# A segment-mean kernel: outputs shifted on chip to fixed addresses and stored plainly, tables built in stages between rows, part of the id sums on ScalarE

## The chip, the cores and the metric

The kernel runs on one core of a Trainium2 chip. The metric is device time in microseconds (us). PE is TensorE, DVE is VectorE, ACT is ScalarE, POOL is GpSimd, SP is SyncE; a trailing q (DVEq, SPq) means the engine's sequencer, which issues DMAs, waits and branches. Every run quoted here was with a granted clock of 1.0 where it was recorded.

## The reference

There are 10 million values with sorted segment ids; the result is the mean of each of 10,000 segments.

```
n, num_segments = 10_000_000, 10000
data = randn(n).astype(float32);  segment_ids = sort(randint(0, num_segments, n))
np.add.at(sums, segment_ids, data)
np.add.at(counts, segment_ids, 1)
return sums / np.maximum(counts, 1)
```

## The kernel before

Each of the 128 partitions takes 78,125 consecutive elements, cut into 98 rows of 800 (the last has 525). On this input a row holds at most one boundary between two segments. The kernel reads every 160th id, gathers by an indirect DMA the 159 ids around the boundary, and gets the boundary's place from their sum. Then, for each row, ACT sums the whole row and DVE sums the part before the boundary (the "split"). From these two numbers per row, small tables give the means.

```
def second_look(a, b):                      # per six rows: the sum of the gathered ids, on DVE
    def s1():
        nc.vector.tensor_reduce(
            out=GS[:, a:b], in_=gt32[:, s : s + b - a, 0 : 2 * W : 2], axis=AX.X, op=ALU.add)
    ...
def total(r):                               # ACT
    nc.scalar.activation(out=junk_a[:, 0:n], in_=d, func=ACT.Copy, accum_out=T[:, r : r + 1])
def split(r):                               # DVE
    nc.vector.scalar_tensor_tensor(
        out=junk_v[:, 0:n], in0=iota[:, 0:n], scalar=KK[:, r : r + 1], in1=d,
        op0=ALU.is_lt, op1=ALU.mult, accum_out=A[:, r : r + 1])
...
def write(o, i):                            # the output's address is in the data: AN
    nc.gpsimd.indirect_dma_start(
        out=out2d[:], out_offset=bass.IndirectOffsetOnAxis(ap=AN[:, i : i + 1], axis=0),
        in_=o[:], in_offset=None)
...
def branch():                               # a general path for inputs of another kind
    with tc.If(nc.values_load(badi[0:1, 0:1], min_val=0, max_val=1) > 0):
        general_path(...)                   # compiled in, never taken on this input
...
after[80].append(verdict)                   # is the fast path allowed?
after[84].append(branch)
after[84].append(tables_a)                  # rows below 66
after[96].append(tables_b)                  # the others but three; first write
...
for r in range(..., NR):
    total(r); split(r)
    for f in after[r]: f()
sums(95, 98); carry(95, 106); table2(); write(out2, 1)
```

A partition's first segment number depends on the data, so `write` stores each partition's 72 and then 8 outputs at addresses from `AN`. The verdict and the tables are three blocks of DVE work, put between the splits.

## Time and profile before

| what | us | where it is read |
|---|---|---|
| time | 214.97, median of 4 runs (214.14 to 215.08) | runs of the same rounds as the changed kernel |
| profiled span | 212.4 | page |
| DVE ends | 201.2 | timeline |
| DVE busy, ACT busy | 149.7, 95.4 | page |

These are lines of the page: the span, the busy time of each engine, the busy tenths in 40 slices of the span (5.3 us each), and the costliest groups (busy time and mean nanoseconds of one, then idle time before them and what ended it).

```profile
span 212.4 us, 1195 instructions
PE 1.6 (1%) x6; PEld 1.4 (1%) x6; DVE 149.7 (70%) x443; ACT 95.4 (45%) x197; POOL 102.2 (48%) x113
...
DVE  5425169848955984993886787589999888999800
ACT  2002047517624753762663664377876598000000
...
DMA  6699999999999999999999999999999990000000
...
L379 DVE SCALAR_TENSOR_TENSOR junk_v<-iota,q_116,data_t 128x800 bf16<-128x800 f32 x98 | 102.4, 1045 | 35.4 <-DMA data_t<-in_data_dram 34.5
L374 ACT ACTIVATE junk_a<-data_t 128x800 bf16<-128x800 f32 x98 | 85.0, 867 | 83.6 <-DMA data_t<-in_data_dram 79.8
L359 DVE TENSOR_REDUCE GS<-GT 128x6 f32<-128x954 int32 (+1 forms) x17 | 18.7, 1103 | 5.1 <-DMA GT<-in_segment_ids_dram,IDX 5.0
```

The DMA row is full up to slice 32, counted from 0 (about 175 us): until then the transfers can limit. DVE is at 8 or 9 tenths from slice 27 to slice 37, beyond the data's end: from about 145 us on DVE is the limit, and it carries a backlog past the last landing. The last two digits of its row are 0: for 11 us nothing computes. The windows view shows the three stretches: DVE is busy 26.7 of 40 us while data come, 9.9 of 10 us after their end, and 1.1 of the last 13; its columns are the stretch, its length, then busy time and count of PE, PEld, DVE, ACT and POOL, the clock, the DMA share and GB/s.

```profile
60.00:100.00 40.00, 0.00 (x0) 0.00 (x0) 26.71 (x72) 19.26 (x40) 22.62 (x24) 1.00 1.05 308
180.00:190.00 10.00, 0.00 (x0) 0.00 (x0) 9.86 (x22) 0.00 (x0) 0.00 (x0) 1.00 0.00 0
200.00:213.00 13.00, 0.00 (x0) 0.00 (x0) 1.14 (x4) 0.00 (x0) 1.24 (x2) 1.00 0.01 4
```

The end of the timeline (start, length, engine, line, operation, and in brackets the idle time before it), and the waits of the SP queue at the kernel's closing line (total us, times, longest):

```profile
200.84 0.40 DVE L582 TENSOR_REDUCE out_141<-sel_135 128x8 f32<-128x232 f32 x1
202.33 0.99 POOL L585 DMA_INDIRECT out_dram<-out_141,AN  x1 [2.09 <-issue]
```

```profile
SPq L703 <- DMA out_dram<-out_141,AN: 27.1, 1, 27.1
SPq L703 <- PEq L703: 6.9, 2, 6.4
```

DVE's last result is there at 201.2; POOL issues the last write at 202.3; it lands at 204.5. From 205.3 on SP waits 6.4 us in one piece, and the span ends at 212.4. The view names PE's sequencer as releaser of that wait.

### The profile page before, as it was taken

The numbers are of one execution on the slowest core, as the hardware profiler recorded it, in microseconds if no ns is written. First come the engines' busy times: TensorE is split into PE (matmuls) and PEld (weight loads), VectorE is DVE, ScalarE is ACT, GpSimd is POOL, SyncE is SP. The second block draws the span as 40 slices with busy tenths as digits, with TensorE's granted clock in tenths as the row PEclk, the third lists the DMA queues.
The fourth block names the chain that finished last, engine by engine and source line by source line (L and its number), as shares of the span: only waits on it lengthen the run. The fifth ranks groups of instructions, "written<-read, shape, count | busy, mean of one in ns | idle before, by whom it ended". The sixth has DMA issues, their size and how long they took to land. (4 is left out here: it accounts for less than half of the span.)

```text
span 212.4 us, 1195 instructions
## 1 busy us (share of the span) xinstructions
PE 1.6 (1%) x6; PEld 1.4 (1%) x6; DVE 149.7 (70%) x443; ACT 95.4 (45%) x197; POOL 102.2 (48%) x113
## 2 busy tenths in 40 slices
PE   0000000100000000000000000000000100000000
PEld 0000000100000000000000000000000000000000
DVE  5425169848955984993886787589999888999800
ACT  2002047517624753762663664377876598000000
POOL 4577756777777427707735752771674000000110
DMA  6699999999999999999999999999999990000000
GB/s 9 36 97 243 250 400 377 145 385 398 270 234 405 397 96 382 391 232 278 403 325 184 396 404 89 402 393 401 415 399 396 406 395 14 0 0 0 7 2 0
DMA packets 74733, 53.39 MB, mean 251 GB/s; under 512 B 65306, under 2 KB 65389, under 8 KB 74720
## 3 DMA queue, kind: packets, MB, share of 16 engines
q1 hardware_dynamic: 69952, 40.51, 66.3%
q0 software_dynamic: 4768, 12.78, 19.7%
q14 instruction: 13, 0.11, 0.1%
HBM read 56.46 MB, written 0.04 MB: 266 GB/s over the span
## 5 line engine op out<-in xcount | busy, mean ns | idle before, releaser
L379 DVE SCALAR_TENSOR_TENSOR junk_v<-iota,q_116,data_t 128x800 bf16<-128x800 f32 x98 | 102.4, 1045 | 35.4 <-DMA data_t<-in_data_dram 34.5
L345 POOL DMA_INDIRECT GT<-in_segment_ids_dram,IDX x98 | 97.9, 999 | 59.9 <-issue 26.5
L374 ACT ACTIVATE junk_a<-data_t 128x800 bf16<-128x800 f32 x98 | 85.0, 867 | 83.6 <-DMA data_t<-in_data_dram 79.8
L359 DVE TENSOR_REDUCE GS<-GT 128x6 f32<-128x954 int32 (+1 forms) x17 | 18.7, 1103 | 5.1 <-DMA GT<-in_segment_ids_dram,IDX 5.0
L585 POOL DMA_INDIRECT out_dram<-out_140,AN x1 | 1.0, 1016 | 37.1 <-DVE out_140 L556 37.1
L374 ACT ACTIVATION_READ_ACCUMULATOR junk_a<-data_t 128x1 f32 x98 | 18.3, 186 | 0.0
L379 DVE DVE_READ_ACCUMULATOR junk_v<-iota,q_116,data_t 128x1 f32 x98 | 8.2, 83 | 0.0
L306 DVE TENSOR_TENSOR eq<-pr 128x40 f32<-128x40 int32 (+3 forms) x11 | 2.1, 192 | 4.3 <-DMA pr<-in_segment_ids_dram 4.3
L364 DVE TENSOR_TENSOR kr<-QQ,GS 128x6 f32<-128x6 f32 (+1 forms) x17 | 2.7, 160 | 0.0
L367 DVE TENSOR_TENSOR q_116<-kr,q_116 128x6 f32<-128x6 f32 (+1 forms) x17 | 2.7, 160 | 0.0
L240 DVE CAST iota<-i_i 128x800 f32<-128x800 int32 x1 | 1.0, 995 | 1.7 <-POOL i_i L239 1.7
L315 DVE TENSOR_SCALAR ST<-jc 128x10 f32<-128x10 f32 (+3 forms) x11 | 2.1, 195 | 0.0
L308 DVE CAST q_116<-pr 128x11 f32<-128x11 int32 (+4 forms) x11 | 2.1, 188 | 0.0
L311 DVE TENSOR_REDUCE jc<-eq 128x10 f32<-128x40 f32 (+3 forms) x11 | 2.0, 186 | 0.0
L319 DVE TENSOR_SCALAR NB<-q_116 128x10 f32<-128x10 f32 (+3 forms) x11 | 2.0, 182 | 0.0
L585 POOL DMA_INDIRECT out_dram<-out_141,AN x1 | 1.0, 988 | 2.1 <-issue 2.1
L336 DVE SCALAR_TENSOR_TENSOR IDX<-NB,pos 128x10 int32<-128x10 f32 (+3 forms) x11 | 1.8, 165 | 0.0
L329 DVE TENSOR_TENSOR pos<-ST,wb 128x10 f32<-128x10 f32 (+3 forms) x11 | 1.8, 165 | 0.0
L330 DVE SCALAR_TENSOR_TENSOR QQ<-q_116,ST 128x10 f32<-128x10 f32 (+3 forms) x11 | 1.8, 161 | 0.0
L312 DVE TENSOR_TENSOR q_116<-q_116 128x10 f32<-128x10 f32 (+3 forms) x11 | 1.7, 158 | 0.0
L374 ACT ACT_TABLE_LOAD x1 | 1.3, 1283 | 0.8 <-PEq L692 0.8
L483 PE MATMUL badp<-bad,ones 128*128 128x1 f32 x2 | 0.6, 362 | 124.3 <-DVE bad L482 124.3
(93 smaller groups left out, 29.0 us busy)
## 6 DMA issues: line engine op xcount, KB each, us to landing
data_t<-in_data_dram SPq DMA_DIRECT2D x48, 800.0 KB, 13.5
GT<-in_segment_ids_dram,IDX POOLq DMA_INDIRECT x98, 6.1
data_t<-in_data_dram SPq DMA_DIRECT2D x1, 662.5 KB, 18.7
pr<-in_segment_ids_dram SPq DMA_DIRECT2D x7, 50.0 KB, 16.9
pr<-in_segment_ids_dram SPq DMA_DIRECT2D x1, 48.0 KB
pr<-in_segment_ids_dram SPq DMA_DIRECT2D x1, 40.0 KB, 5.7
pr<-in_segment_ids_dram SPq DMA_DIRECT2D x1, 30.0 KB, 5.1
pr<-in_segment_ids_dram SPq DMA_DIRECT2D x1, 21.0 KB, 3.3
```

The lines of the kernel that those rows point to most:

```text
L306: nc.vector.tensor_tensor(out=eq, in0=in0b, in1=in1b, op=ALU.is_equal)
L308: nc.vector.tensor_copy(out=V[:, a:e], in_=pr32[:, a:e, 0])
L311: nc.vector.tensor_reduce(out=jc, in_=eq, axis=AX.X, op=ALU.add)
L315: nc.vector.tensor_scalar(out=ST[:, a:b], in0=jc, scalar1=float(S), scalar2=float(1 + W), op0=ALU.mult, op1=ALU.add,)
L319: nc.vector.tensor_scalar(out=NB[:, a:b], in0=BT[:, a:b], scalar1=-1.0, scalar2=1.0, op0=ALU.mult, op1=ALU.add)
L345: nc.gpsimd.indirect_dma_start(out=GT[:, r % RING, :], out_offset=None, in_=ids2d[:], in_offset=bass.IndirectOffsetOnAxis(ap=IDX[:, r : r ...
L359: nc.vector.tensor_reduce(out=GS[:, a:b], in_=gt32[:, s : s + b - a, 0 : 2 * W : 2], axis=AX.X, op=ALU.add)
L364: nc.vector.tensor_sub(out=kr, in0=QQ[:, a:b], in1=GS[:, a:b])
L367: nc.vector.tensor_mul(out=KK[:, a:b], in0=kr, in1=BT[:, a:b])
L374: nc.scalar.activation(out=junk_a[:, 0:n], in_=d, func=ACT.Copy, accum_out=T[:, r : r + 1])
L379: nc.vector.scalar_tensor_tensor(out=junk_v[:, 0:n], in0=iota[:, 0:n], scalar=KK[:, r : r + 1], in1=d, op0=ALU.is_lt, op1=ALU.mult, accum_ ...
L585: nc.gpsimd.indirect_dma_start(out=out2d[:], out_offset=bass.IndirectOffsetOnAxis(ap=AN[:, i : i + 1], axis=0), in_=o[:], in_offset=None,)
```

## The change

The intent: take work off DVE, spread what stays into its idle time, and shorten the end. The core of the diff:

```
-    def write(o, i):
-        nc.gpsimd.indirect_dma_start(out=out2d[:], out_offset=...AN..., in_=o[:], in_offset=None)
+    def place(c0, c1):          # shift a partition's table by its own delta (0..12), by a mask
+        def s1(): nc.vector.tensor_tensor(out=shf[:, c0:c1, :], in0=view(tab[:, c0 : c0 + 1], [[1, n], [1, ND]]),
+                      in1=view(dm[:, 0:1], [[0, n], [1, ND]]), op=ALU.mult)
+        def s2(): nc.vector.tensor_reduce(out=own[:, c0:c1], in_=shf[:, c0:c1, :], axis=AX.X, op=ALU.add)
+    def late_out():             # after the last split: only the last 4 rows' terms
+        ...
+        nc.vector.tensor_reduce(out=OUT[:, CL:NO], in_=prodL, axis=AX.X, op=ALU.add)
+        for i, (src, dst) in enumerate(own_outputs(OUT, out2d[0:1, :])):      # four plain stores
+            (nc.scalar if i % 2 else nc.sync).dma_start(out=dst, in_=src)
+    def add_ids(r):             # rows below ON_ACT = 66
+        nc.scalar.activation(out=junk_a[:, 0:W], in_=gt32[:, r % RING, 0 : 2 * W : 2], func=ACT.Copy,
+                             accum_out=GS[:, r : r + 1])
...
-    after[CHECK_AT].append(verdict)
-    after[IF_AT].append(tables_a)
-    after[C2 + 1].append(tables_b)
+    put(46, counts(0, 48))
+    put(52, sums(0, 48) + table(0, 8))
+    put(70, counts(48, 72))
+    put(max(bounds[NG - 1] - X_LOOK, 0) + 5, keys(48, NX)[1:] + check(), 2)
+    IF_AT = 83
+    put(76, select(8, 13))
+    put(77, sums(48, 72) + table(8, 13) + place(0, 40), 2)
     after[IF_AT].append(branch)
+    put(IF_AT + 1, [first_out])
+    put(IF_AT + 2, select(13, NT1 // 4))
+    put(91, counts(72, NX), 3)
+    put(93, ext_sums() + late_select(), 6)
+    put(93, sums(72, RL) + table(13, NT1 // 4) + place(40, NO) + early_out(), 16)
```

`put` appends one step after one row, the next step after the next row, or a few at a time. Further: the gathers' look-ahead moves by two rows and that of the probes (every 160th id) by three, the last tile is loaded in two pieces, and the first six outputs have a store of their own (`first_out`).

## The prediction

> **What bounds the kernel now.** Up to about 144 us the transfers: the windows view gives a DMA share of 1.0 or more from 15 us on, with DVE busy 82%, 67%, 75% of 30-60, 60-100, 100-140 us; DVE and ACT wait for data_t (waits view: 34.5 and 79.8 us). From row 68 on (144.2 us) DVE: data come at about 1.1 us a row, a split costs DVE 1.09 us (timeline), so every other DVE op is lag never made good: verdict 161.9 to 167.4 (5.5 us), first tables 172.0 to 178.9 (7 us), second tables 193.2 to 198.9 (5.7 us), id sums 1.06 us per six rows. The last tile lands at about 177.4 us (issue 158.5 plus 18.7), but DVE ends at 201.2. Then the tail: 1.1 us until POOL issues, 1.0 us of POOL, 2.2 us to landing (205.5), 6.9 us of epilogue to 212.4.
>
> **What the change does.**
> 1. Id sums of rows 0 to 65 go to ScalarE: 11 reduces of 1.1 us off DVE, in the stage where DVE waits for data, so I credit about nothing. On ACT each costs an estimated 0.47 us (slope of its 800- and 525-column forms plus the accumulator read): 1.46 us a row with the total, against about 1.75 us a row of arriving data. ACT keeps up.
> 2. Verdict and tables are spread between splits. The work stays on DVE, but independent ops after a split start every 0.07 to 0.12 us instead of a dependent 0.2 or more. Tables of rows below 48 move into idle time.
> 3. New DVE work: shifting (two multiplies, two reduces of about 510 elements, 0.69 us each) and a 92-column table. Between rows 93 and 94 about 6.3 us still runs in one block.
> 4. The end after the last split falls to an estimated 1.3 us.
> 5. Plain stores replace the indirect write. [...] I take 2.6 us from DVE's end to landing instead of 4.3.
> 6. DMA bytes are unchanged; probes come a few rows later; data end within 1 us of 177.4.
>
> **The sum.** I replayed the new DVE order with durations and arrivals from the trace (the same replay of the old order ends at 199.6 plus 1.1 us of branch waits; true 201.2). DVE lag passes 4 us at row 75, 9 us at row 82, 12 us at row 93; DVE ends at about 197.5. DVE gains 3.7 us, the tail 1.7: 5.4 of the 24 us that DVE runs after the last tile. Span about 207, time **208.8 us**, range 205.3 to 211.8. Chances: faster by over 2% 0.77, within 2% 0.21, slower 0.02.
>
> **What would show it.** Timeline: row 68's split near 144 us; DVE without gaps after about row 70; a 6 us block of tables before the last four splits, near 185 to 191; DVE end 196 to 199; stores landing under 3 us later. Lines: id reduces on DVE about 6 us instead of 18.7; ACT busy about 125 us.
>
> **What would make it wrong.** Data earlier around rows 66 to 72 (gathers shift by two rows) end DVE earlier by as much. Interleaved small ops dearer than 0.1 us each, later. The two reads of the fallback tiles wait for the skipped branch's semaphores, which the DMA queue gives only as tiles 44 and 48 land (168.7 and 177.4 us): were DVE quicker than I think, it would stall there, and could not end below about 184. The epilogue may change without the POOL write.

The 2.6 us is the estimate; what the trace shows is 2.2 us from the start of the last indirect write's issue to its landing. The sum: 3.7 us of DVE and 1.7 us of tail (4.3 less 2.6) make 5.4 us, from a span of 212.4 us to about 207.

## The result

| | before | after |
|---|---|---|
| time, us | 214.97 (214.14 to 215.08) | 205.64 (205.27 to 205.75) |
| profiled span, us | 212.4 | 204.0 |
| DVE ends, us | 201.24 | 200.09 |
| DVE's end to the span's end, us | 11.2 | 3.9 |
| DVE busy, ACT busy, us | 149.7, 95.4 | 139.5, 124.2 |

The ratio is 0.9571, with a 95% interval of 0.9544 to 0.9598: faster. A ratio here is the mean time of one kernel's fast runs over that of the other's of the same rounds, so not quite the ratio of the medians. The lines that answer to those of before:

```profile
span 204.0 us, 1430 instructions
PE 1.6 (1%) x6; PEld 1.4 (1%) x6; DVE 139.5 (68%) x454; ACT 124.2 (61%) x329; POOL 100.3 (49%) x112
...
DVE  5520924864488488458748848884999997499992
ACT  2013497996499699679959847653779668910000
...
DMA  5699999999999999999999999999999999300000
...
L416 DVE SCALAR_TENSOR_TENSOR junk_v<-iota,q_121,data_t 128x800 bf16<-128x800 f32 x98 | 102.1, 1042 | 41.5 <-DMA data_t<-in_data_dram 37.0
L411 ACT ACTIVATE junk_a<-data_t 128x800 bf16<-128x800 f32 x98 | 85.0, 867 | 33.8 <-DMA data_t<-in_data_dram 27.8
L381 ACT ACTIVATE junk_a<-GT 128x159 bf16<-128x159 int32 x66 | 22.8, 346 | 20.5 <-DMA GT<-in_segment_ids_dram,IDX 18.6
```

Two things in the DVE row were not in the plan. Its last digit is 2, where before it had two zeros: the empty end is gone. And a 7 and a 4 stand between the nines, at slices 33 and 34 (168 to 178 us), in the middle of the stretch where DVE limits.

The timeline shows that dip as one hole, just after the branch over the fallback (L780). "issue" means that the profile shows nothing the engine waited for.

```profile
171.31 1.05 DVE L416 SCALAR_TENSOR_TENSOR junk_v<-iota,q_121,data_t 128x800 bf16<-128x800 f32 x1 [0.30 <-DVEq L780]
172.28 0.08 DVE L416 DVE_READ_ACCUMULATOR junk_v<-iota,q_121,data_t 128x1 f32 x1
172.28 0.21 DVE L730 SCALAR_TENSOR_TENSOR out_156<-tab,nflag,fb_158 1x6 f32<-1x6 f32 x1
176.14 1.05 DVE L416 SCALAR_TENSOR_TENSOR junk_v<-iota,q_121,data_t 128x800 bf16<-128x800 f32 x1 [3.65 <-issue]
...
199.74 0.35 DVE L747 TENSOR_REDUCE OUT<-prodL 128x21 f32<-128x189 f32 x1
```

So DVE, expected 3.7 us earlier, was 1.15 us earlier, and the end, expected 1.7 us shorter, was 7.3 us shorter (11.2 less 3.9). That the total still fell inside the predicted range is luck: one term was too large and the other too small. For the span 5.4 us of gain were predicted and 8.4 measured; for the time, 208.8 us and 205.64.

The end, in the SP queue's waits:

```profile
SPq L860 <- DMA out_dram<-OUT: 0.7, 2, 0.5
SPq L860 <- PEq L860: 0.7, 2, 0.5
```

The piece of 6.4 us is now 0.5. The groups of the closing line show what it was. Here the columns are count, minimum, median and maximum ns, and first and last start. The first fence is before, the second after:

```profile
L703 POOLq DRAIN  x3: 40/113/9161, 202.4 to 212.1; - x3
```

```profile
L860 POOLq DRAIN  x3: 40/107/8077, 167.2 to 203.7; - x3
```

In both kernels POOL ends its program with one long DRAIN, of 9161 and 8077 ns. Before, it began at 202.4 us, with the last indirect write, and the whole core waited for it until 211.6. After, POOL's last work is a gather that ends at 164.2 us and its part of the branch, up to 167.2; its DRAIN runs from 167.2 to 175.3 us, where nobody waits for it.

### The profile page after: what moved, and what is told of

The parts are those of the page before. It is cut to its first block, busy times and chain, and to the rows that moved or that the text cites. A ratio compares the mean times of both kernels' runs of the same rounds, so it can differ in the third digit from the quotient of the medians.

```text
span 204.0 us, 1430 instructions
## 1 busy us (share of the span) xinstructions
PE 1.6 (1%) x6; PEld 1.4 (1%) x6; DVE 139.5 (68%) x454; ACT 124.2 (61%) x329; POOL 100.3 (49%) x112
## 5 line engine op out<-in xcount | busy, mean ns | idle before, releaser
L381 ACT ACTIVATE junk_a<-GT 128x159 bf16<-128x159 int32 x66 | 22.8, 346 | 20.5 <-DMA GT<-in_segment_ids_dram,IDX 18.6
L381 ACT ACTIVATION_READ_ACCUMULATOR junk_a<-GT 128x1 f32 x66 | 12.3, 186 | 0.0
L400 DVE TENSOR_TENSOR kr<-QQ,GS 128x6 f32<-128x6 f32 (+2 forms) x17 | 2.7, 161 | 10.8 <-ACT junk_a L381 10.8
L394 DVE TENSOR_REDUCE GS<-GT 128x6 f32<-128x954 int32 (+2 forms) x6 | 6.2, 1032 | 0.0
L403 DVE TENSOR_TENSOR q_121<-kr,q_121 128x6 f32<-128x6 f32 (+2 forms) x17 | 2.8, 167 | 0.0
L673 DVE TENSOR_REDUCE tab<-sel 128x32 f32<-128x384 f32 (+2 forms) x3 | 1.6, 534 | 0.1
```

What stands on the lines that cost most here:

```text
L381: nc.scalar.activation(out=junk_a[:, 0:W], in_=gt32[:, r % RING, 0 : 2 * W : 2], func=ACT.Copy, accum_out=GS[:, r : r + 1],)
L394: nc.vector.tensor_reduce(out=GS[:, c:e], in_=gt32[:, s : s + e - c, 0 : 2 * W : 2], axis=AX.X, op=ALU.add)
L400: nc.vector.tensor_sub(out=kr, in0=QQ[:, a:b], in1=GS[:, a:b])
L403: nc.vector.tensor_mul(out=KK[:, a:b], in0=kr, in1=BT[:, a:b])
```

## The experiments

Theory for the end: the 7 us came from POOL's closing DRAIN, because POOL no longer issues the last DMA. Rival: any plain store has a short end for another reason (fewer waits on the write, a shorter POOL program). Theory for the hole, a guess that no view shows: the DVE's instruction stream is being refilled after the jump over the fallback (below: the "refill"). Rivals: the store of the first outputs, or the small operation before it, stalls DVE; or the interleaved operations do. Times are medians; ratios are to the kernel before in the same rounds (its medians were 214.3, 213.9, 214.0 and 214.2 us in the four batches).

### One small store of the changed kernel issued by POOL

```
-            (nc.scalar if i % 2 else nc.sync).dma_start(out=dst, in_=src)
+            [nc.sync, nc.scalar, nc.sync, nc.gpsimd][i].dma_start(out=dst, in_=src)
```

> The changed kernel with the smallest of its four last stores (15 elements) issued on GpSimd's queue instead of ScalarE's. Theory (the end of the program waits for a GpSimd drain of 8 to 9 us that starts after GpSimd's last DMA; in the kernel before it ran from 202.4 to 211.6 us, in the changed one from 167.2 to 175.3, out of sight): the drain moves to about 201.5 to 210, the span grows by 6 to 7.5 us, time 211.5 to 213. Rival (the end became short because the scatter by index and its descriptors went, or because one wait per store is cheap): time within 1 us of 205.6.

Measured: 211.66 us (211.11 to 212.01), ratio 0.9865 (0.9838 to 0.9891). Only one store of 15 values changed its queue, and 6 us came back. The drain and SP's wait:

```profile
L860 POOLq DRAIN  x3: 44/113/8753, 200.6 to 210.0; - x3
```

```profile
SPq L860 <- PEq L860: 6.9, 2, 6.4
```

The wait of 6.4 us is back to the tenth. DVE's end hardly moved (200.4 against 200.1). So the end depends on when POOL issues its last DMA, and not on the write being indirect.

### The kernel before, with plain stores and nothing else

Wrong results: the two stores go to fixed addresses without the shift.

```
-        nc.gpsimd.indirect_dma_start(...AN...)
+        nc.sync.dma_start(out=bass.AP(z.tensor, z.offset + off, [[c, n], [1, c]]), in_=o[0:n, :])
```

> The kernel before with its two indirect writes replaced by two plain stores of the same tiles to fixed addresses on the sync queue. Result wrong on purpose (outputs land at shifted addresses). Theory (the tail is nearly the whole gain): DVE still ends near 201.2, stores land by 204, no drain behind them; span about 204.7, time 206 to 207.5, that is almost all of the change's 9.3 us. Rival, my prediction (the store is worth 1.7 us, DVE's work the rest): time 212.5 to 213.5.

Measured: 205.59 us (205.40 to 206.16), ratio 0.9598 (0.9572 to 0.9623). That is the time of the whole change, and a little under what I had expected. DVE ends at 201.1 as before; the span is 203.7.

```profile
L702 POOLq DRAIN  x3: 40/107/8077, 169.0 to 203.5; - x3
```

So moving the last write off POOL is worth nearly all of the net gain. All the rest of the change, for which the page counts 235 more instructions, paid back what it cost and no more. Why, the next runs tell.

### Without the branch

```
-    after[IF_AT].append(branch)
```

> The changed kernel without the conditional fallback (this data never takes it, so the result stays right). Theory (the 3.65 us hole of DVE at 172.5 to 176.1 us is an instruction refill after the jump over the fallback[...]): the hole goes, with the 0.3 us of the branch itself; DVE ends near 196.2 instead of 200.1, time 201.3 to 202. Rival (the hole is a wait of the small first_out operation's tile or store): the hole stays, time within 0.7 us of 205.6.

Measured: 203.38 us (202.91 to 204.97), ratio 0.9511 (0.9464 to 0.9559). The hole is gone; DVE ends at 196.7. I had expected 201.3 to 202; data came later in this run (row 68's split at 143.8 us, against 143.2), its end took 4.4 us instead of 3.9, and its times scatter more than others. The branch is needed for the hole; this run alone doesn't tell how it makes it.

### The first outputs' store moved away from the branch

```
-    put(IF_AT + 1, [first_out])
+    put(92, [first_out])
```

> The changed kernel with the small first_out operation and its store moved from after row 84 to after row 92; the branch stays at row 83. Refill theory: a hole of 3 to 4 us stays, at nearly the same time (about 172 to 176) and one or two instructions further on; time within 0.5 us of 205.6. Rival (first_out's waits make the hole): no hole at 172 us, time 201.5 to 202.5 if it doesn't come back at row 92.

Measured: 205.75 us (204.93 to 206.54), ratio 0.9585 (0.9554 to 0.9615). The hole stays, now between a split and the read of its own accumulator:

```profile
174.02 1.05 DVE L416 SCALAR_TENSOR_TENSOR junk_v<-iota,q,data_t 128x800 bf16<-128x800 f32 x1
177.75 0.08 DVE L416 DVE_READ_ACCUMULATOR junk_v<-iota,q,data_t 128x1 f32 x1 [2.68 <-issue]
```

These two are one line of the kernel, and no operand of another engine or DMA lies between them. The rival falls: the store of the first outputs isn't the cause. What stays the same is the count of instructions behind the jump: the fourth one stalls in both kernels.

### No id sums on ScalarE

```
-ON_ACT = 66
+ON_ACT = 0
```

> The changed kernel with all id sums back on DVE (one number: 66 to 0). My prediction credited the move of rows 0 to 65 with about nothing, as DVE waits for data there: row 68's split stays within 0.7 us of 143.2, DVE's end within 0.7 us of 200.1, time 205 to 206.5, with about 12 us more DVE busy time. Rival (the move is worth its 12 us of DVE work, or a good part): time 208 or more.

Measured: 202.15 us (201.91 to 202.83), ratio 0.9459 (0.9438 to 0.9479). This missed: I expected no gain over the change (ratio 0.9571), and it is 1.2% faster. The hole is gone, although the branch is there, and DVE ends at 195.8 with 10.6 us more work (busy 150.1). The edit adds 11 reduces, with their waits, ahead of the branch; it moves every later instruction of DVE along.

### More id sums on ScalarE

```
-ON_ACT = 66
+ON_ACT = 90
```

> The changed kernel with the id sums of rows 66 to 89 on ScalarE too (66 to 90). These four reduces of 1.06 us stand in the stage where DVE is the limit, so all of it should count: DVE ends 4.2 us earlier, near 195.9, time 201 to 202. ScalarE pays about 24 times 0.47, 11 us, and has slack; if it becomes the limit instead, DVE waits for its totals before the late tables and the gain is under 2 us.

Measured: 200.11 us (199.69 to 200.33), ratio 0.9356 (0.9341 to 0.9372), DVE's end 194.0, which is 1 to 2 us better than expected. With four reduces fewer ahead of the jump the hole comes later behind it, after seven DVE instructions instead of three, and is shorter:

```profile
170.34 1.03 DVE L416 SCALAR_TENSOR_TENSOR junk_v<-iota,q,data_t 128x800 bf16<-128x800 f32 x1
172.57 0.08 DVE L416 DVE_READ_ACCUMULATOR junk_v<-iota,q,data_t 128x1 f32 x1 [1.20 <-issue]
```

The jump (the event that closes the branch on DVE's sequencer) is at 167.5 us here and at 171.1 in the changed kernel. The holes end at 172.57 and 176.14: 5.1 and 5.0 us after the jump. A transfer that starts at the jump and takes 5 us, and for which DVE waits in the end, would fit this; no view shows such a wait.

### The branch seven rows later

```
-    IF_AT = 83
+    IF_AT = 90
...
-    put(IF_AT + 2, select(13, NT1 // 4))
+    put(85, select(13, NT1 // 4))
```

> The changed kernel with the branch (and first_out) seven rows later, after row 90, when the data stream has ended. Refill theory: the hole moves behind the branch to about 180 us and shrinks to 2 us or less[...]; time 203.5 to 204.8. If the hole's length doesn't depend on traffic: a hole of 3.5 us at the new place, time within 0.5 us of 205.6. ScalarE's own wait at the branch is not on the path in either case.

Measured: 201.77 us (201.67 to 202.11), ratio 0.9436 (0.9420 to 0.9451). No hole, DVE's end 196.0: both forecasts missed. The jump (180.1 us) is now after the last data. It also has more instructions ahead of it, so this run cannot tell an effect of the traffic from another place in the stream. That a refill waits behind data was not shown. Whether the 5 us depend on the DMA traffic stays open (the count after the runs has a hint).

### The staging undone

The verdict goes back into one block at row 80, and the tables of rows below 72 into one block after the branch; the outputs' shift and the id sums stay as changed.

```
-    put(46, counts(0, 48)) ... put(77, sums(48, 72) + table(8, 13) + place(0, 40), 2)
+    put(80, keys(48, NX)[1:] + check(), 99)
+    put(84, counts(0, 48) + counts(48, 72) + sums(0, 48) + ... + table(0, 13) + place(0, 40), 99)
```

> The changed kernel with the staging undone: the verdict in one block after row 80, and counts, sums and tables of rows below 72 in one block after row 84, as in the kernel before; the last tables stay where they are. Theory (work moved into DVE's waits or between splits is worth what it takes in a block): the block costs about 6 us at row 84 and the verdict about 2.5 us more than spread; DVE ends 5 to 8 us later, time 210.5 to 213.5. Rival (spreading is worth little, since the work stays on DVE): time under 208.

Measured: 208.14 us (207.38 to 208.30), ratio 0.9720 (0.9696 to 0.9745), DVE's end 202.4, no hole. My expectation compared it with the changed kernel, which has the hole, and so was too high; the rival's bound (below 208) wasn't met either. Against kernels without the hole (196.1 for the next one), the staging is worth about 6 us of DVE's end. That is more than the 3.7 us of net gain that I had predicted for DVE.

### Eleven idle instructions early in the stream

```
+    padt = cpool.tile([P, 11], FP32, name="padt")
+    for i in range(11):
+        put(6, [lambda i=i: nc.vector.memset(padt[:, i : i + 1], 0.0)])
```

> The changed kernel with eleven one-column memsets of an unused tile on DVE after row 6, where DVE waits for data; as many instructions as the id sums that came back in the run with all sums on DVE. Theory ([...]holes stood 3 instructions behind the jump in the changed kernel, 3 with first_out moved, 7 with four reduces fewer before it): [...]the hole goes, DVE ends near 196, time 201.6 to 202.6. Rival (moving the id sums to ScalarE itself cost the 3.5 us): the hole stays, time within 0.7 us of 205.6.

What the runs had shown is that the stall moves with the count of instructions ahead of the jump; the guess was that eleven more take it away.

Measured: 201.74 us (201.61 to 201.82), ratio 0.9427 (0.9411 to 0.9443). The memsets compute nothing that anyone reads and are at row 6, about 135 us before the branch. The kernel that has more work is faster: its ratio is lower by 0.0144, or 3.1 us of the 214 us of before, and its profiled span by 4.0 us (200.0). The hole of 3.65 us is gone and DVE ends at 196.1:

```profile
172.07 0.21 DVE L730 SCALAR_TENSOR_TENSOR out<-tab,nflag,fb 1x6 f32<-1x6 f32 x1
172.21 1.03 DVE L416 SCALAR_TENSOR_TENSOR junk_v<-iota,q,data_t 128x800 bf16<-128x800 f32 x1
173.18 0.07 DVE L416 DVE_READ_ACCUMULATOR junk_v<-iota,q,data_t 128x1 f32 x1
```

For the instructions at the jump the edit changes their place in DVE's stream, by eleven, and next to nothing else: the jump is at 170.9 us, against 171.1.

### A combination, with 17 idle instructions

ON_ACT 98, X_SUM 9, and 17 memsets at row 6.

> The changed kernel with all id sums on ScalarE (98, look-ahead 9 rows) and seventeen such memsets[...]. Against the run with sums up to row 90 on ScalarE (200.1 us): 1.2 us of hole and 1.5 us of the last two reduces less on DVE; DVE ends near 191.5, time 197 to 198.2. If ScalarE becomes late with the totals of rows 72 to 93, DVE waits before the last tables and the time is 199 or more.

Measured: 201.88 us (201.43 to 202.47), ratio 0.9428 (0.9410 to 0.9446). Missed. The hole is there and longer than ever, after only two instructions:

```profile
174.00 0.21 DVE L730 SCALAR_TENSOR_TENSOR out<-tab,nflag,fb 1x6 f32<-1x6 f32 x1 [4.02 <-issue]
```

I had counted the reduces that go away, but not the waits that are instructions of their own and go with them. The padding had put the stall back where it was. The jump is at 168.7 us, the end of the hole 5.3 us later.

### The last rows' order undone

```
-    put(93, ext_sums() + late_select(), 6)
-    put(93, sums(72, RL) + table(13, NT1 // 4) + place(40, NO) + early_out(), 16)
+    put(97, ...the same two...)
```

> The changed kernel with the last tables moved behind the last split, so that the last four rows are no longer added on their own. DVE is the limit there and all data have landed by 177 us, so the order of its work should not matter: time within 0.6 us of 205.6. Rival (adding four rows one by one shortens the end): 6 us more, 211 or so.

Measured: 205.01 us (204.81 to 205.36), ratio 0.9587 (0.9571 to 0.9603), DVE's end 199.2; the hole is as in the changed kernel (3.66 us). By the ratio (0.9571 for the change) adding the last four rows by themselves gains nothing that shows. DVE still has a backlog then: the same work is done before or after the last splits.

### The combination, with 30 idle instructions

> All id sums on ScalarE as in the run before (201.9 us), with thirty memsets instead of seventeen: there I had not counted the wait instructions that went away with the reduces, and [...]a hole of 4.0 us ending 5.2 us after it. [...] Theory: no hole, DVE ends near 192.8, time 197.4 to 198.4. If the hole has another cause it stays and the time is within 0.7 us of 201.9.

Measured in five rounds: 197.66 us (197.51 to 198.42), ratio 0.9235 (0.9210 to 0.9259), no hole, correct, DVE's end 191.9, DVE busy 134.5 and ACT 138.1. It beats both kernels; the changed one by 0.0336 in the ratio, 7.2 us of 214. Its page:

```profile
span 195.8 us, 1535 instructions
...
DVE  4620814976179568728854982968489989999991
```

### A count after the runs

The compiled programs allow a check that cost no run. I numbered DVE's instructions in the order in which they stand, waits and the skipped fallback included, and counted each split twice, since its accumulator read is an instruction of its own. "Stalls" is the number of the instruction that ends the hole in the trace.

| kernel | first number behind the jump | stalls | hole, us | ends after the jump, us |
|---|---|---|---|---|
| after | 576 | 580 | 3.65 | 5.0 |
| with a POOL store | 576 | 580 | 3.62 | 5.0 |
| first outputs late | 576 | 580 | 2.68 | 5.0 |
| last rows' order undone | 576 | 580 | 3.66 | 5.0 |
| 17 idle instructions, ON_ACT 98 | 577 | 580 | 4.02 | 5.3 |
| ON_ACT 90 | 560 | 569 | 1.20 | 5.1 |
| 11 idle; 30 idle; branch late; ON_ACT 0 | 587; 590; 604; 620 | none | 0 | |
| staging undone | 552 | none | 0 | |

In five kernels the same number stalls, 580, whichever operation stands there: a split, an accumulator read, or the first outputs. Where the jump lands beyond 580 there is no hole. Where it lands 28 before (staging undone), there is none either: there DVE began its 23rd operation behind the jump only at 174.4 us, 5.4 us after the jump (169.0 us), when the 5.0 to 5.3 us of the table would be over. One kernel doesn't fit, ON_ACT 90, which stalls 11 instructions early by this count; I can't explain that one.

The traces' DMA records show what may be waited for: packets of 8 KB on the queue named "instruction" (14 of them, 0.11 MB, on the changed kernel's page). These lines of the DMA view are from the changed kernel (window 174 to 174.5 us) and from the late branch (180.5 to 181); they give the packets, MB, and share of the engines' time.

```profile
q14 instruction: 1, 0.01, 4.1%
```

```profile
q14 instruction: 1, 0.01, 5.7%
```

For four of the six kernels with a hole the windows of the DMA view place such a packet (after, POOL store, ON_ACT 90, 17 idle instructions): it starts 3.0 to 3.3 us after DVE's jump, and the stalled instruction begins about 1.6 us after its end (from 174.55 to 176.14 us in the changed kernel); for ON_ACT 90 too, where the packet comes before the hole. Kernels without a hole have such packets all the same (3 between 168 and 180 us with 11 idle instructions, 4 between 165 and 180 us with 30), but there DVE doesn't stall. With the late branch, after the data's end, one comes 0.6 us after the jump, 2.4 to 2.7 us sooner than in those four. That hints at the traffic, but doesn't show it: it is one run, and the records don't say which engine a packet is for.

## Why the prediction was right or wrong

**The time fell inside the range, near its low end (205.3), but the parts of the sum were wrong.** DVE was to bring most of the gain; the end brought it.

1. *"then the tail: 1.1 us until POOL issues, 1.0 us of POOL, 2.2 us to landing (205.5), 6.9 us of epilogue to 212.4", and step 5, "2.6 us from DVE's end to landing instead of 4.3"*: this step failed. It took what follows the landing as fixed and credited 1.7. The end gave 7.3. By the landings in the traces, the last write lands 2.7 us after DVE's end (202.8) instead of 3.3 (204.5), which is 0.6 us of gain; what follows the landing shrank from 7.9 to 1.2 us, which is 6.7. (The 205.5 was a misreading: the view counts the 2.2 us from the start of POOL's 1.0 us, not from its end. So the landing had less to give than the 1.7 credited.) What follows the landing was mostly SP's wait, 6.4 us in one piece, while POOL drained for 9.2 us; the POOL store put 6.4 us of wait back, and plain stores in the kernel before took them away. The text had named the chance ("The epilogue may change without the POOL write"), without a size. The size could have been asked of the trace: POOL's DRAIN of 9161 ns stood in the groups of the closing line.

   The landing itself came as predicted, 2.7 us after DVE's end for 2.6. Where the DMA view of the changed kernel tells it, these stores, issued by SP and ACT, landed 2.1 to 2.4 us after their issue. But four stores, two on each queue, took 1.5 to 1.6 us to issue; that is probably why the end is 3.9 us, where the kernel before with one plain store in its place has 2.7.

2. *"DVE ends at about 197.5"*: off by 2.6 us. The replay held up to the branch: row 68's split stood at 143.16 us ("near 144"). *"DVE without gaps after about row 70"* failed: one hole of 3.65 us. Without it DVE would have ended at 196.4 (200.1 less 3.65); the padded kernel shows 196.1; with row 68 about 0.8 us early, the replay agrees within about half a us. The missed term is a stall behind the jump over the fallback. In the runs the instructions just behind the jump run at once (after a gap of 0.30 us), and the stall comes two to seven DVE operations later, until 5.0 to 5.3 us after the jump. That it hangs on the place in the stream is shown (11 memsets, and the table above). That it is a fetch of instructions is the guess, to which the packets above would fit; it is not shown, and the profile itself says only "issue".

3. *Step 1, "I credit about nothing" for the id sums on ScalarE*: right for these 66 rows. Without holes, DVE's end is 195.8 with none of them on ACT and 196.1 with 66. DVE waits for data in that stage. Moving also those of rows 66 to 89, in the stage where DVE limits, ended DVE at 194.0, even with a hole of 1.2 us. ACT kept up, as predicted (busy 124.2 against "about 125").

4. *Step 2, the spread of verdict and tables*: right in kind, worth about 6 us (202.4 less 196.1). In the net it met 1.1 us (202.36 against 201.24 of the kernel before, both with blocks), which I put down to the new output work, and 3.65 us of hole. Roughly: −6.2 + 1.1 + 3.65 = −1.45, measured −1.15.

5. *"a 6 us block of tables before the last four splits"*: there it is, from 188.8 to 194.6. It can't be told apart in time from the same block after the last split (ratios 0.9587 and 0.9571).

All told: the end −7.3, DVE −1.15, together the 8.4 us by which the profiled span shrank. The medians differ by 9.3 us. The other 0.9 us comes from which execution was profiled: one of 214.16 us before, 0.8 under the median, and one of 205.75 after, 0.1 over it.

## What to carry to other kernels

Read the end of a kernel as its own stage, and ask of each piece which engine's closing work it is: a wait that looks like an epilogue can be GpSimd's drain. It lasted 9161 ns behind the indirect write, 8753 behind the direct one and 8077 where the branch came last, and ended 8.1 to 8.3 us after GpSimd's last own instruction in these three kernels. By that measure, an estimate, it is out of sight if that instruction comes some 10 us before the end. Where a kernel has a jump over much code, look for an idle stretch with no releaser shortly behind it, and compare variants only when both have it or both have not: here eleven idle instructions, placed early, were worth 3 to 4 us. And a total that comes out right proves no term of its sum; check each term against the trace.
